# A two-layer attention and gated-MLP trunk on one core: spatial mixing with split float32r operands, output bias loaded per group

## The chip, the core and the metric

The kernel runs on one core of one Trainium2 chip. The core has five engines that run side by side: TensorE (PE, matmuls; its weight loads are listed as PEld), VectorE (DVE), ScalarE (ACT), GpSimd (POOL) and SyncE (SP, which here only issues transfers). The metric is the device time of one execution in microseconds. Before the change it is 2550.82 us, the median of three runs (2549.76 to 2550.91).

## The reference

Two layers work on x of 2048 rows by 1024 columns. Each layer projects x to 4,864 columns (queries, keys, values, gates and the gMLP halves), runs sliding-window attention on one branch and the gMLP on the other, and merges both by gates; an output projection, a residual and a LayerNorm follow. The change touches the gMLP's position mixing and the place where the output bias comes from. Of the reference that is:

```python
vn = layer_norm(v, ln_g, ln_b).reshape(B, nc, CHUNK, GMLP_GROUPS, GMLP_GROUP_DIM)
w = jnp.where(causal[None], w_s, jnp.zeros_like(w_s))
mixed = jnp.einsum('gts,bcsgd->bctgd', w, vn) + b_s.T[None, None, :, :, None]
y_g = gelu(u) * mixed * silu(z_g)
...
out = jnp.einsum('bsd,de->bse', merged, w_out[l]) + b_out[l]
x = layer_norm(ALPHA * x + out, ln_g[l], ln_b[l])
```

All data are float32. There are 4 mixing groups of 128 columns, and 16 chunks of 128 positions.

## The kernel before

The rows are worked in 4 groups of 512 (NG), each of 4 blocks of 128 (NB); both layers together make eight passes through `group(l, g, xs)`. Big products are made of float32r operands: a value is split into a high part (rounded to float32r) and a low part (the rest), and high*high, low*high and high*low are added in PSUM (`accum_t`, `accum_w`, L177 through `mm`). `hilo` does such a split: ACT casts the high part (L201), DVE subtracts it (L202). Weights arrive in units of 1024 columns. In the first group of a layer a unit is split by ACT (L136) and DVE (L137) and its two halves are kept in DRAM; in later groups the halves are loaded from there.

The order of work is the order in which the program is written, with one addition: small tasks stand in a queue (`side`), and `step` takes one after every few big matmuls (`pace`). So the attention's scores, transposes and products, and the gMLP's LayerNorm and mixing, are strewn among the matmuls of the input projection. A scheduler then orders each engine's queue; an engine works its queue strictly in that order, and a wait at its head holds everything behind it.

Position mixing of one pass: `v_norm` (L514) normalizes each of four blocks in place; then four tasks `mix_task(gi)` follow, one for each mixing group. Each takes one PSUM bank from the pool `ps_at` (3 banks, in rotation; scores and attention output use the same pool), makes four float32 matmuls (L522), and DVE evacuates the bank (L525: times `g_col`, plus `bias2`), multiplies by the gate (L530) and splits the result into the branch product's operand (`hilo`: L201, L202). The task just ahead of them, `pv_task(3)`, is the last attention product (L443), evacuated at L448.

The profile counts a float32 matmul as two records: 128 instructions at L522 show as 256.

The tiles `t` of the pool `tp` (15 buffers, in rotation) hold short-lived values of 128x512; `bo_b` (the output bias, copied to all partitions) is a constant, loaded by POOL once per layer (L254) and read at L664, where the residual is scaled.

Of the kernel before, what the change touches and what calls it, by code (L numbers as in the profile page):

```python
# [14 lines left out]
P = 128  # L15
D = 1024
# [33 lines left out]
def trunk_kernel(ctx, tc, xg, xt, wu, bcol, bvg, sinks, lngc, lnb, wsp, bsp, bout, ln_g, ln_b,  # L50
# [161 lines left out]
    sink = [const.tile([P, HEADS], F32, name=f"sink{l}") for l in range(DEPTH)]  # L212
    nsink = [const.tile([P, HEADS], F32, name=f"nsink{l}") for l in range(DEPTH)]
    vg_b = const.tile([P, GW], F32, name="vg_b")
    wsT = const.tile([P, NGR, P], F32, name="wsT")
    bias2 = const.tile([P, NGR, P], F32, name="bias2")
    bo_b = const.tile([P, D], F32, name="bo_b")
    lg_b = const.tile([P, D], F32, name="lg_b")
    lb_b = const.tile([P, D], F32, name="lb_b")
    kept = [[dram.tile([P, 2, 1024], F32, name=f"kept{l}_{n}") for n in range(NUNITS)] for l in range(DEPTH)]  # L220
# [12 lines left out]
    def mix_consts(l):  # L233
        if l > 0:
            pool.dma_start(out=vg_b, in_=bvg[l].partition_broadcast(P))
        pool.dma_start(out=wsT, in_=wsp[l])
        pool.affine_select(out=wsT, in_=wsT, pattern=[[0, NGR], [1, P]], compare_op=ALU.is_ge,
                           fill=0.0, base=0, channel_multiplier=-1)
        t = TT()
        pool.dma_start(out=t, in_=lnb[l].partition_broadcast(P))  # L240
        t2 = TT()
        pool.dma_start(out=t2, in_=bsp[l].partition_broadcast(P))

        def go():
            ps = AT([P, NGR, P])
            for gi in range(NGR):
                pe.matmul(ps[:, gi, :], lhsT=t[:, gi * P:(gi + 1) * P], rhs=wsT[:, gi, :],
                          start=True, stop=True)
            dve.tensor_tensor(out=bias2.rearrange("p g t -> p (g t)"),
                              in0=ps.rearrange("p g t -> p (g t)"), in1=t2, op=ALU.add)  # L250
        return always, go

    def out_consts(l):
        pool.dma_start(out=bo_b, in_=bout[l].partition_broadcast(P))  # L254
        pool.dma_start(out=lg_b, in_=ln_g[l].partition_broadcast(P))
        pool.dma_start(out=lb_b, in_=ln_b[l].partition_broadcast(P))

# [48 lines left out]
    def group(l, g, xs):  # L306
# [204 lines left out]

        def v_norm(b):
            def go():
                dve.tensor_scalar(out=hv[b], in0=hv[b], scalar1=mv[:, b, 0:1], scalar2=rs[:, b, :],  # L514
                                  op0=ALU.subtract, op1=ALU.mult)
            return always, go

        def mix_task(gi):
            def go():
                ps = AT([P, NB, P])  # L520
                for b in range(NB):
                    pe.matmul(ps[:, b, :], lhsT=hv[b][:, gi * P:(gi + 1) * P], rhs=wsT[:, gi, :],  # L522
                              start=True, stop=True)
                t = TT([P, NB, P])
                dve.scalar_tensor_tensor(  # L525
                    out=t, in0=ps, scalar=g_col[l][:, gi:gi + 1],
                    in1=bias2[:, gi, :].unsqueeze(1).to_broadcast([P, NB, P]),
                    op0=ALU.mult, op1=ALU.add)
                t2 = t.rearrange("p b t -> p (b t)")
                dve.tensor_tensor(out=t2, in0=t2, in1=szg[gi], op=ALU.mult)  # L530
                ys[4 + gi] = hilo(Y, t2)
# [62 lines left out]
        for b in range(NB):  # L594
            for h in range(2):
                row = g * NB + b
                src = xt[row * P:(row + 1) * P] if l == 0 else x1[g][:, b, :]
                sp.dma_start(out=rt[b][h], in_=src[:, h * T:(h + 1) * T])
        st = S([P, NB, 2, 6], "st2")
        mv = S([P, NB, 2], "mv2")  # L600
        rs = S([P, NB, 1], "rs2")
# [44 lines left out]
        for h in range(2):  # L646
# [12 lines left out]
            for u in range(1 if tail else 4):  # L659
                W = next_unit(T)  # L660
                for b in range(NB):
                    accum_w(banks[b], W, ms, u, b)
                    if u == 0:
                        dve.scalar_tensor_tensor(out=rt[b][h], in0=rt[b][h], scalar=ALPHA,  # L664
                                                 in1=bo_b[:, h * T:(h + 1) * T], op0=ALU.mult, op1=ALU.add)
            if tail:
                Ws = [next_unit(T) for _ in range(3)]
                for b in range(NB):
# [123 lines left out]
```

## Time and profile before

| What | Value |
|---|---|
| Median of three runs | 2550.82 us |
| The profiled execution | 2550.75 us |
| Its span, first to last instruction | 2549.1 us |
| Granted TensorE clock, mean over the span | 0.996 |
| TensorE busy | 2521.4 us (99%) |
| VectorE busy | 1436.6 us (56%) |
| ScalarE busy | 691.3 us (27%) |

Outside the span lie 1.65 us of the profiled execution. Matmuls overlap in the records (the end of one lies behind the start of the next), so what one costs TensorE is read from the distance of starts, and not from its duration.

### The profile page before, as it was taken

What the parts mean: (1) busy time and instruction counts of PE and PEld (TensorE: products, weight loads), DVE (VectorE), ACT (ScalarE), POOL (GpSimd) and SP (SyncE); (2) the same over time, 40 slices, a digit from 0 to 9 for tenths busy, and PEclk for the clock granted to TensorE, in tenths of its full rate; (3) what the DMA queues carried; (4) which work ended last, traced back from release to release, by engine and by line L of the source; (5) the groups of instructions that cost most, each with busy time, mean ns of one, the idle gap of its engine ahead of it and who ended that gap; (6) DMA issues with size and microseconds to landing.
All of it is one profiled execution on the core that took longest, in us unless ns stands there. A gap on an engine that the chain in (4) does not pass through costs nothing.

```text
span 2549.1 us, 32409 instructions
## 1 busy us (share of the span) xinstructions
PE 2521.4 (99%) x12176; PEld 2093.3 (82%) x12176; DVE 1436.6 (56%) x3752; ACT 691.3 (27%) x1322; POOL 431.1 (17%) x448
## 2 busy tenths in 40 slices
PE   8999999999999999999999999999999999999997
PEld 6888888888888888888878888888888888888886
DVE  7963568213782137725789577772467625586214
ACT  4443233111421114211154332421115111141110
POOL 1120041100411004210041100420003200132002
PEclk9999999999999999999999999999999999999999
DMA  8788964457554575556676897555565456655454
GB/s 322 252 293 298 330 247 168 171 192 263 201 179 169 194 264 198 186 187 222 248 273 235 292 322 287 203 180 186 212 229 200 181 183 213 235 195 179 170 196 165
DMA packets 116108, 568.39 MB, mean 223 GB/s; under 512 B 12112, under 2 KB 28528, under 8 KB 60528
## 3 DMA queue, kind: packets, MB, share of 16 engines
q1 hardware_dynamic: 109776, 546.35, 60.6%
q0 software_dynamic: 6176, 19.97, 2.2%
q8 instruction: 96, 1.57, 0.2%
q14 instruction: 60, 0.49, 0.1%
HBM read 436.25 MB, written 130.02 MB: 222 GB/s over the span
## 4 chain that ended last, share of the span: by engine, by line
PE 92%; DVE 3%; issue 2%; DMA 1%; ACT 1%; POOL 0%; SPq 0%; POOLq 0%; DVEq 0%; ACTq 0%
PE mm L177 86%; PE at L443 2%; PE at L374 2%; PE at L522 1%; DMA wr<-in_wu 1%; DVE t L288 1%; DVE w L137 1%; DVE y L664 0%; DMA b<-in_score_bias 0%; ACT y L641 0%; POOL rs L608 0%; DMA y<-in_xt 0%; DVE x L202 0%; ACT w L136 0%; SPq L264 0%
## 5 line engine op out<-in xcount | busy, mean ns | idle before, releaser
L177 PE MATMUL mm<-x,w 128*128 128x512 f32 x6528 | 1519.8, 391 | 8.6 <-ACT x L201 6.2
L177 PEld LDWEIGHTS mm<-x,w 128*128 128x128 f32 x6528 | 1220.0, 188 | 266.0 <-ACT x L201 7.0
L177 PE MATMUL mm<-y,w 128*128 128x512 f32 x1536 | 353.6, 389 | 0.0
L177 PE MATMUL mm<-w,m 128*128 128x512 f32 x1536 | 349.8, 389 | 0.2 <-DVE y L651 0.2
L177 PEld LDWEIGHTS mm<-w,m 128*128 128x128 f32 x1536 | 288.3, 188 | 60.4 <-DVE y L651 0.6
L177 PEld LDWEIGHTS mm<-y,w 128*128 128x128 f32 x1536 | 288.3, 188 | 59.7
L424 DVE STREAM_TRANSPOSE t<-t 32x128 f32<-32x128 f32 x1024 | 309.3, 302 | 14.1
L583 POOL TENSOR_TENSOR t<-t,t 128x512 f32<-128x512 f32 x64 | 85.0, 1328 | 996.8 <-DVE t L582 930.8
L137 DVE TENSOR_TENSOR w<-wr,w 128x1024 fp32r<-128x1024 f32 x108 | 148.0, 1371 | 139.7 <-ACT w L136 138.8
L551 ACT ACTIVATE t<-mm,bcol 128x512 f32<-128x512 f32 x128 | 88.2, 689 | 427.1 <-PE mm L177 427.1
L579 DVE TENSOR_TENSOR t<-t,mm 128x512 f32<-128x512 f32 x64 | 43.7, 683 | 273.4 <-PE mm L177 273.3
L177 PE MATMUL mm<-w,x 128*128 128x512 f32 x768 | 190.6, 392 | 0.0
L288 DVE STREAM_TRANSPOSE t<-t 32x128 f32<-32x128 f32 x512 | 154.9, 302 | 50.4 <-DMA t<-x 43.1
L136 ACT CAST w<-wr 128x1024 fp32r<-128x1024 f32 x108 | 113.2, 1048 | 209.9 <-DMA wr<-in_wu 114.7
L177 PEld LDWEIGHTS mm<-w,x 128*128 128x128 f32 x768 | 139.1, 189 | 25.5
L429 POOL TENSOR_SCALAR_AFFINE_SELECT t<-t 128x512 f32<-128x512 f32 x64 | 44.7, 698 | 519.4 <-DVE t L424 508.7
L201 ACT CAST m<-t 128x512 fp32r<-128x512 f32 x64 | 39.8, 621 | 291.1 <-POOL t L583 291.1
L406 ACT ACTIVATE t<-t,negm 128x128 f32<-128x128 f32 x256 | 99.3, 389 | 50.1 <-DVE negm L396 49.7
L651 DVE TENSOR_TENSOR y<-y,mm 128x512 f32<-128x512 f32 x64 | 43.9, 687 | 120.0 <-PE mm L177 120.0
L382 DVE CUSTOM_DVE_ANT_0 t<-at,b 128x256 f32<-128x256 f32 (+1 forms) x256 | 97.2, 412 | 20.8 <-PE at L374 18.0
L641 ACT ACTIVATE y<-y,nm,rs 128x512 f32<-128x512 f32 x56 | 41.1, 805 | 183.3 <-DVE nm L682 183.1
L494 ACT ACTIVATE m<-mm,bcol 128x512 f32<-128x512 f32 x64 | 44.1, 689 | 156.9 <-PE mm L177 156.7
(94 smaller groups left out, 1760.8 us busy)
## 6 DMA issues: line engine op xcount, KB each, us to landing
w<-kept SPq DMA_DIRECT2D x324, 1024.0 KB, 4.8
kept<-w SPq DMA_DIRECT2D x108, 1024.0 KB, 4.9
wr<-in_wu SPq DMA_DIRECT2D x108, 512.0 KB, 6.0
t<-in_xg SPq DMA_DIRECT2D x32, 256.0 KB, 6.1
y<-in_xt SPq DMA_DIRECT2D x32, 256.0 KB, 6.2
x<-y POOLq DMA_DIRECT2D x32, 256.0 KB, 4.7
t<-x SPq DMA_DIRECT2D x32, 256.0 KB, 5.6
y<-x SPq DMA_DIRECT2D x32, 256.0 KB, 6.4
```

The costliest lines, as they stand in the source:

```text
L136: act.copy(out=t[:, 0, :], in_=r)
L137: dve.tensor_tensor(out=t[:, 1, :], in0=r, in1=f(t)[:, 0, :], op=ALU.subtract)
L177: pe.matmul(o, lhsT=a, rhs=b, start=start, stop=stop, skip_group_check=skip)
L288: dve.transpose(out=outs[k][32 * i:32 * i + 32, :, 32 * r:32 * r + 32], in_=tiles[k][32 * r:32 * r + 32, :, 32 * i:32 * i + 32])
L374: pe.matmul(ps[:, j, :], lhsT=q[c][j][:, b * P:(b + 1) * P], rhs=KT[a][j][:, b * P:b * P + 2 * P], start=a == 0, stop=a == 1)
L382: dve.tensor_tensor_reduce(out=t[:, j, lo:], in0=ps[:, j, lo:], in1=b8[:, 2 * c + j, lo:], scale=1.0, scalar=NEG, op0=ALU.add, op1=ALU.max ...
L406: act.activation(out=w, in_=w, func=AF.Exp, bias=negm[:, bb, j:j + 1], scale=HD ** -0.5, accum_out=sums[:, bb, j:j + 1])
L424: dve.transpose(out=cur_[32 * i:32 * i + 32, :, 32 * r:32 * r + 32], in_=w[32 * r:32 * r + 32, :, 32 * i:32 * i + 32])
L429: pool.affine_select(out=prev_, in_=cur_, pattern=[[0, 4], [-1, P]], compare_op=ALU.is_gt, fill=0.0, base=0, channel_multiplier=1)
L443: pe.matmul(po[j * HD:(j + 1) * HD, b * P:(b + 1) * P], lhsT=VT[:, b + kb, j * HD:(j + 1) * HD], rhs=A["p"][b // 2][1 - kb][:, 2 * (b % 2) ...
L551: act.activation(out=t, in_=ps, func=AF.Sigmoid, bias=bias(i))
L583: pool.tensor_tensor(out=sa, in0=sa, in1=sg, op=ALU.add)
```

## The change

The mixing weights are split once per layer into a high and a low part that lie side by side (`ws2`, 4 groups of 2 x 128 columns). Each normalized block is split too (`hv[b] = hilo(M, n)`). A mixing task now makes, for each block, one float32r matmul of the block's high part with both halves of the weights (128x256, L529) and one of its low part with the high half (128x128, L531). The 128x256 results of two blocks fill a bank, so a task takes two banks of `ps_at`, where it took one, and DVE adds both halves of each bank (L534, L538), where it had one instruction. The output bias is no constant any more: each pass loads two tiles of 128x512 through the SP queue (L613) into the pool `tp`.

```diff
--- before.py
+++ after.py
@@ -212,9 +212,8 @@
     sink = [const.tile([P, HEADS], F32, name=f"sink{l}") for l in range(DEPTH)]
     nsink = [const.tile([P, HEADS], F32, name=f"nsink{l}") for l in range(DEPTH)]
     vg_b = const.tile([P, GW], F32, name="vg_b")
-    wsT = const.tile([P, NGR, P], F32, name="wsT")
+    ws2 = const.tile([P, NGR, 2, P], F32R, name="ws2")
     bias2 = const.tile([P, NGR, P], F32, name="bias2")
-    bo_b = const.tile([P, D], F32, name="bo_b")
     lg_b = const.tile([P, D], F32, name="lg_b")
     lb_b = const.tile([P, D], F32, name="lb_b")
     kept = [[dram.tile([P, 2, 1024], F32, name=f"kept{l}_{n}") for n in range(NUNITS)] for l in range(DEPTH)]
@@ -233,6 +232,7 @@
     def mix_consts(l):
         if l > 0:
             pool.dma_start(out=vg_b, in_=bvg[l].partition_broadcast(P))
+        wsT = TT([P, NGR, P])
         pool.dma_start(out=wsT, in_=wsp[l])
         pool.affine_select(out=wsT, in_=wsT, pattern=[[0, NGR], [1, P]], compare_op=ALU.is_ge,
                            fill=0.0, base=0, channel_multiplier=-1)
@@ -248,10 +248,11 @@
                           start=True, stop=True)
             dve.tensor_tensor(out=bias2.rearrange("p g t -> p (g t)"),
                               in0=ps.rearrange("p g t -> p (g t)"), in1=t2, op=ALU.add)
+            act.copy(out=ws2[:, :, 0, :], in_=wsT)
+            dve.tensor_tensor(out=ws2[:, :, 1, :], in0=wsT, in1=f(ws2)[:, :, 0, :], op=ALU.subtract)
         return always, go
 
     def out_consts(l):
-        pool.dma_start(out=bo_b, in_=bout[l].partition_broadcast(P))
         pool.dma_start(out=lg_b, in_=ln_g[l].partition_broadcast(P))
         pool.dma_start(out=lb_b, in_=ln_b[l].partition_broadcast(P))
 
@@ -511,21 +512,32 @@
 
         def v_norm(b):
             def go():
-                dve.tensor_scalar(out=hv[b], in0=hv[b], scalar1=mv[:, b, 0:1], scalar2=rs[:, b, :],
+                n = TT()
+                dve.tensor_scalar(out=n, in0=hv[b], scalar1=mv[:, b, 0:1], scalar2=rs[:, b, :],
                                   op0=ALU.subtract, op1=ALU.mult)
+                hv[b] = hilo(M, n)
             return always, go
 
         def mix_task(gi):
             def go():
-                ps = AT([P, NB, P])
-                for b in range(NB):
-                    pe.matmul(ps[:, b, :], lhsT=hv[b][:, gi * P:(gi + 1) * P], rhs=wsT[:, gi, :],
-                              start=True, stop=True)
                 t = TT([P, NB, P])
-                dve.scalar_tensor_tensor(
-                    out=t, in0=ps, scalar=g_col[l][:, gi:gi + 1],
-                    in1=bias2[:, gi, :].unsqueeze(1).to_broadcast([P, NB, P]),
-                    op0=ALU.mult, op1=ALU.add)
+                cs = slice(gi * P, (gi + 1) * P)
+                for b0 in range(0, NB, 2):
+
+                    ps = AT([P, 2, 2, P])
+                    for b in range(2):
+                        pe.matmul(ps[:, b], lhsT=hv[b0 + b][0][:, cs], rhs=ws2[:, gi], start=True,
+                                  stop=False, skip_group_check=True)
+                        pe.matmul(ps[:, b, 0, :], lhsT=hv[b0 + b][1][:, cs], rhs=ws2[:, gi, 0, :],
+                                  start=False, stop=True, skip_group_check=True)
+                    to = t[:, b0:b0 + 2, :]
+                    dve.scalar_tensor_tensor(
+                        out=to, in0=ps[:, :, 0, :], scalar=g_col[l][:, gi:gi + 1],
+                        in1=bias2[:, gi, :].unsqueeze(1).to_broadcast([P, 2, P]),
+                        op0=ALU.mult, op1=ALU.add)
+                    dve.scalar_tensor_tensor(
+                        out=to, in0=ps[:, :, 1, :], scalar=g_col[l][:, gi:gi + 1], in1=to,
+                        op0=ALU.mult, op1=ALU.add)
                 t2 = t.rearrange("p b t -> p (b t)")
                 dve.tensor_tensor(out=t2, in0=t2, in1=szg[gi], op=ALU.mult)
                 ys[4 + gi] = hilo(Y, t2)
@@ -596,6 +608,9 @@
                 row = g * NB + b
                 src = xt[row * P:(row + 1) * P] if l == 0 else x1[g][:, b, :]
                 sp.dma_start(out=rt[b][h], in_=src[:, h * T:(h + 1) * T])
+        bo_b = [TT() for _ in range(2)]
+        for h in range(2):
+            sp.dma_start(out=bo_b[h], in_=bout[l][h * T:(h + 1) * T].partition_broadcast(P))
         st = S([P, NB, 2, 6], "st2")
         mv = S([P, NB, 2], "mv2")
         rs = S([P, NB, 1], "rs2")
@@ -662,7 +677,7 @@
                     accum_w(banks[b], W, ms, u, b)
                     if u == 0:
                         dve.scalar_tensor_tensor(out=rt[b][h], in0=rt[b][h], scalar=ALPHA,
-                                                 in1=bo_b[:, h * T:(h + 1) * T], op0=ALU.mult, op1=ALU.add)
+                                                 in1=bo_b[h], op0=ALU.mult, op1=ALU.add)
             if tail:
                 Ws = [next_unit(T) for _ in range(3)]
                 for b in range(NB):
```

On TensorE, second pass of the first layer, the first mixing task among the input projection's matmuls; before (`at` is the PSUM bank, `m` a normalized block):

```order
L177 MATMUL mm_4118<-x_2571,w_3984 128x512 x2
L177 MATMUL mm_4118<-x_2572,w_3984 128x512
L522 MATMUL at_4125<-wsT,m_3438 128x128
L522 MATMUL at_4125<-wsT,m_3440 128x128
L522 MATMUL at_4125<-wsT,m_3442 128x128
L522 MATMUL at_4125<-wsT,m_3444 128x128
L177 MATMUL mm_4118<-x_2584,w_3984 128x512 x2
L177 MATMUL mm_4118<-x_2585,w_3984 128x512
```

After (`ws_103` is `ws2`; the blocks are pairs of high and low part, 4114 and 4115, 4132 and 4133, and so on):

```order
L177 MATMUL mm_4195<-x_2628,w_4041 128x512 x2
L177 MATMUL mm_4195<-x_2629,w_4041 128x512
L529 MATMUL at_4203<-ws_103,m_4114 128x256
L531 MATMUL at_4203<-ws_103,m_4115 128x128
L529 MATMUL at_4203<-ws_103,m_4132 128x256
L531 MATMUL at_4203<-ws_103,m_4133 128x128
L529 MATMUL at_4210<-ws_103,m_4145 128x256
L531 MATMUL at_4210<-ws_103,m_4146 128x128
L529 MATMUL at_4210<-ws_103,m_4157 128x256
L531 MATMUL at_4210<-ws_103,m_4158 128x128
L177 MATMUL mm_4195<-x_2641,w_4041 128x512 x2
L177 MATMUL mm_4195<-x_2642,w_4041 128x512
```

The task has kept its place between the same big matmuls; it makes eight instructions and fills two banks (4203 and 4210).

On VectorE, the same pass, from the evacuation of the last attention product (L448) on; before:

```order
L328 COPY vt<-vt 128x128
L448 TENSOR_TENSOR t_4108<-at_4091,m_3630 128x512
L525 SCALAR_TENSOR_TENSOR t_4130<-at_4125,gcol_96,bias_104 128x512
L202 TENSOR_TENSOR y_4111<-t_4108,y_4110 128x512
L530 TENSOR_TENSOR t_4130<-t_4130,m_3698 128x512
L525 SCALAR_TENSOR_TENSOR t_4149<-at_4144,gcol_96,bias_104 128x512
L202 TENSOR_TENSOR y_4134<-t_4130,y_4133 128x512
L530 TENSOR_TENSOR t_4149<-t_4149,m_3747 128x512
```

After (L449 is the same evacuation; 4203 and 4210 are the banks of the first task, 4230 and 4237 of the second):

```order
L449 TENSOR_TENSOR t_4185<-at_4168,m_3687 128x512
L534 SCALAR_TENSOR_TENSOR t_4202<-at_4203,gcol_96,bias_104 128x256
L202 TENSOR_TENSOR y_4188<-t_4185,y_4187 128x512
L538 SCALAR_TENSOR_TENSOR t_4202<-at_4203,gcol_96,t_4202 128x256
L534 SCALAR_TENSOR_TENSOR t_4202<-at_4210,gcol_96,bias_104 128x256
L538 SCALAR_TENSOR_TENSOR t_4202<-at_4210,gcol_96,t_4202 128x256
L542 TENSOR_TENSOR t_4202<-t_4202,m_3755 128x512
L534 SCALAR_TENSOR_TENSOR t_4229<-at_4230,gcol_96,bias_104 128x256
L534 SCALAR_TENSOR_TENSOR t_4229<-at_4237,gcol_96,bias_104 128x256
L202 TENSOR_TENSOR y_4219<-t_4202,y_4218 128x512
L538 SCALAR_TENSOR_TENSOR t_4229<-at_4230,gcol_96,t_4229 128x256
L538 SCALAR_TENSOR_TENSOR t_4229<-at_4237,gcol_96,t_4229 128x256
```

A bank is free when its L538 is done. That of the second task's first bank (4230) now stands behind a split's subtraction (L202) that waits for ACT.

On VectorE, first pass of the first layer, ahead of the mixing's first evacuation (L137 is a weight split, which waits for ACT's cast of the same unit; `vt` the attention's carried values); before:

```order
L137 TENSOR_TENSOR w_1586<-wr_1496,w_1586 128x1024
L137 TENSOR_TENSOR w_1622<-wr_1548,w_1622 128x1024
L328 COPY vt<-vt 128x128
L137 TENSOR_TENSOR w_1703<-wr_1590,w_1703 128x1024
L448 TENSOR_TENSOR t_1654<-at_1637,m_1118 128x512
L202 TENSOR_TENSOR y_1657<-t_1654,y_1656 128x512
L525 SCALAR_TENSOR_TENSOR t_1672<-at_1667,gcol_96,bias_104 128x512
```

After (4 normalizations at L516, here of blocks one to four, and the subtractions of their splits at L202):

```order
L137 TENSOR_TENSOR w_1588<-wr_1496,w_1588 128x1024
L516 TENSOR_SCALAR t_1600<-m_903,mv_1365,rs_1366 128x512
L516 TENSOR_SCALAR t_1613<-m_905,mv_1365,rs_1366 128x512
L516 TENSOR_SCALAR t_1625<-m_907,mv_1365,rs_1366 128x512
L202 TENSOR_TENSOR m_1603<-t_1600,m_1602 128x512
L137 TENSOR_TENSOR w_1639<-wr_1550,w_1639 128x1024
L202 TENSOR_TENSOR m_1616<-t_1613,m_1615 128x512
L202 TENSOR_TENSOR m_1628<-t_1625,m_1627 128x512
L516 TENSOR_SCALAR t_1647<-m_909,mv_1365,rs_1366 128x512
L329 COPY vt<-vt 128x128
L202 TENSOR_TENSOR m_1650<-t_1647,m_1649 128x512
L137 TENSOR_TENSOR w_1741<-wr_1592,w_1741 128x1024
```

Before, the normalizations stood further up, ahead of the attention's transposes. Now they stand between the weight splits next to the mixing; the subtraction of the fourth block (1650) is the last one, behind a weight split and two subtractions that wait for ACT.

## Rows read from the trace of the kernel before

**Rows 1.** The page: busy time, share of the span, instructions

```profile
PE 2521.4 (99%) x12176; PEld 2093.3 (82%) x12176; DVE 1436.6 (56%) x3752; ACT 691.3 (27%) x1322; POOL 431.1 (17%) x448
```

**Rows 2.** Timeline of TensorE, pass two: start us, us, line, operation, count

```profile
471.90 1.05 PE L522 MATMUL at<-wsT,m 128*128 128x128 f32 x8
472.71 1.85 PE L177 MATMUL mm<-x,w 128*128 128x512 f32 x7
474.40 1.05 PE L522 MATMUL at<-wsT,m 128*128 128x128 f32 x8
...
476.66 1.05 PE L522 MATMUL at<-wsT,m 128*128 128x128 f32 x8
...
479.96 10.69 PE L177 MATMUL mm<-x,w 128*128 128x512 f32 x46
490.49 11.04 PE L177 MATMUL mm<-y,w 128*128 128x512 f32 x48
501.37 9.00 PE L177 MATMUL mm<-x,w 128*128 128x512 f32 x39
```

**Rows 3.** Timeline of TensorE, scores of the second layer, float32r, 256 columns

```profile
1304.47 0.28 PE L374 MATMUL at<-ka,m 128*128 128x256 f32 x1
...
1304.94 2.23 PE L177 MATMUL mm<-x,w 128*128 128x512 f32 x9
```

**Rows 4.** Weight loads by form: shapes, count | busy us, mean ns | idle

```profile
L443 PEld LDWEIGHTS at<-t,vt 128*64 128x64 f32 x1024 | 55.2, 137 | 11.3 <-issue 7.8 <-POOL t L429 1.8 <-POOL t L431 1.8
...
L522 PEld LDWEIGHTS at<-wsT,m 128*128 128x128 f32 x256 | 33.5, 191 | 2.5
```

**Rows 5.** VectorE by form, same columns

```profile
L525 DVE SCALAR_TENSOR_TENSOR t<-at,gcol,bias 128x512 f32<-128x512 f32 x32 | 23.9, 748 | 11.6 <-PE at L522 11.6
...
L530 DVE TENSOR_TENSOR t<-t,m 128x512 f32<-128x512 f32 x32 | 22.0, 688 | 0.9
...
L626 DVE SCALAR_TENSOR_TENSOR y<-y,mv,lg_b 128x256 f32<-128x256 f32 x2 | 1.0, 479 | 0.0
```

**Rows 6.** ScalarE by form, same columns

```profile
L201 ACT CAST y<-t 128x512 fp32r<-128x512 f32 x64 | 39.7, 620 | 150.2 <-DVE t L448 100.3 <-DVE t L530 49.8
```

**Rows 7.** Timeline of VectorE, pass two

```profile
472.99 0.75 DVE L525 SCALAR_TENSOR_TENSOR t<-at,gcol,bias 128x512 f32<-128x512 f32 x1 [1.77 <-PE at L522]
473.66 0.68 DVE L202 TENSOR_TENSOR y<-t,y 128x512 fp32r<-128x512 f32 x1
```

**Rows 8.** Window, pass two: PE, PEld, DVE, ACT, POOL busy, clock, DMA

```profile
458.00:469.00 11.00, 11.00 (x55) 8.93 (x55) 0.00 (x1) 1.51 (x3) 2.57 (x2) 1.00 0.53 192
```

**Rows 9.** Timeline of VectorE, pass one

```profile
157.63 1.22 DVE L137 TENSOR_TENSOR w<-wr,w 128x1024 fp32r<-128x1024 f32 x1 [3.52 <-ACT w L136]
...
162.25 1.22 DVE L137 TENSOR_TENSOR w<-wr,w 128x1024 fp32r<-128x1024 f32 x1 [3.26 <-ACT w L136]
163.39 0.68 DVE L448 TENSOR_TENSOR t<-at,m 128x512 f32<-128x512 f32 x1
```

**Rows 10.** Timeline of TensorE, pass one

```profile
159.85 1.05 PE L522 MATMUL at<-wsT,m 128*128 128x128 f32 x8
...
162.12 1.05 PE L522 MATMUL at<-wsT,m 128*128 128x128 f32 x8
```

**Rows 11.** Timeline of VectorE, pass five (first of the second layer)

```profile
1423.94 0.68 DVE L448 TENSOR_TENSOR t<-at,m 128x512 f32<-128x512 f32 x1
```

**Rows 12.** Timeline of TensorE, pass five

```profile
1424.67 1.05 PE L522 MATMUL at<-wsT,m 128*128 128x128 f32 x8
```

**Rows 13.** Timeline of TensorE, start of the second layer

```profile
1295.10 0.39 PE L374 MATMUL at<-ka,m 128*128 128x256 f32 x1 [1.96 <-DVE m L462]
...
1297.16 0.58 PE L374 MATMUL at<-ka,m 128*128 128x256 f32 x1 [1.56 <-DVE m L462]
```

**Rows 14.** Window around that place, same columns

```profile
1295.00:1320.00 25.00, 23.34 (x107) 19.65 (x108) 23.44 (x72) 13.59 (x29) 9.39 (x11) 0.86 0.91 332
```

**Rows 15.** DMA issues: out<-in, engine, count, KB each, median us to landing

```profile
bo_b<-in_bout POOLq DMA_DIRECT2D x2, 512.0 KB, 6.7
```

## The prediction, made before the changed kernel ran

> **What bounds the kernel now.** I read the page's table of engines first: TensorE is busy for 99% of the span, no other engine for more than 56% [rows 1]. So the time is TensorE's work plus its few waits, and a change is worth what it does to the one or the other; work on VectorE or ScalarE counts only where TensorE comes to wait for it. Next I read TensorE's timeline around one pass's mixing, for prices by distance of starts. Forty-eight big matmuls take 501.37 - 490.49 = 10.88 us, 0.2267 us each. From the first mixing record (471.90) to 490.49 lie 18.59 us with four mixing tasks and 7, 6, 7 and 46 big matmuls; 66 x 0.2267 = 14.96 us, and 3.63 us remain, 0.907 us a task or 0.113 us for each of its eight records [rows 2]. There are 32 tasks (8 passes of 4), 29 us in all.
>
> **What the change does to TensorE's work.** A task's eight float32 records become four float32r matmuls of 256 columns and four of 128. The first kind stands in the trace, as the scores: four take 1304.94 - 1304.47 = 0.47 us, 0.1175 us each [rows 3]. The second, a float32r matmul of 128 columns, does not. Below, it could cost half of the 256-column one, 0.059 us. Above, it could cost as much as the whole float32 matmul of this size, two records, 0.227 us. Between them is the float32 record itself, which has the same columns and the same 128x128 weights: 0.113 us. Loads of weights speak for that middle: a load of 64 columns is recorded with 137 ns and one of 128 with 191 ns [rows 4], so 64 columns more are 54 ns, and 128 columns are by estimate 108 ns of loading. Each small matmul still needs a load of its own, and a matmul can't follow faster than the loads do. I take 0.113. The task is then 4 x (0.1175 + 0.113) = 0.92 us, against 0.907: +0.5 us in 32 tasks. At 0.059 it is 0.706 us (-6.4 us in all), at 0.227 it is 1.378 us (+15.1 us).
>
> The Trainium skill speaks against this middle: "TensorE: Matmul & The Clock Gate", section "Back-to-back issue gap", gives some 81 ns for a matmul of 128 columns in a stream of load and matmul pairs. By it the task would be 4 x (117.5 + 81) = 794 ns, 3.6 us less than now in 32 tasks. The float32 records at 113 ns can't decide it, as they may be slow by their type and not by their loads; no row here is a float32r one of this size.
>
> **What it adds on VectorE and ScalarE.** Before, a task's VectorE work is 0.748 + 0.688 us and a subtraction of about the same 0.69 [rows 5, 7]: 2.13 us. Now the 0.748 becomes four instructions of 128x256. The nearest row of that size and kind takes 0.479 us from SBUF [rows 5], and half of 0.748 would be 0.374; I take 0.48, so the task is 3.30 us. With the split of the blocks (one subtraction each) VectorE gets 32 x (1.17 + 0.69) = 60 us more, ScalarE 32 casts of 0.620 us, 20 us [rows 6]. In most of a pass that is hidden: VectorE does nothing from 458 to 469 us, just before the mixing [rows 8], and in pass two the normalizations and casts fit there. What isn't hidden is the speed of evacuation. TensorE reaches a task every 2.3 to 2.5 us (474.40 - 471.90, 476.66 - 474.40) [rows 2]. VectorE's 3.30 us, with a wait for ScalarE's cast between multiplication and subtraction, is slower than that. Before, a task took one bank of three; now it takes two. So the second bank of the third task is the first of the second task, and the second bank of the second task the first of the first.
>
> **The waits, place by place.** An instruction on VectorE follows some 0.08 us before the end recorded for the one ahead (473.66 after 472.99 + 0.75) [rows 7], and some 0.1 us after it where it needs its result (my estimate). Pass two: the first bank is full at about 472.54 and evacuation begins. By the order shown above it goes L534, subtraction, L538, L534, L538, multiplication, to 475.8 us; then two L534 for the second task and a subtraction that waits for a cast until 476.5; the L538 that frees its first bank ends at 477.6. TensorE wants that bank 0.46 us into its third task, at 476.66 + 0.46 = 477.1 [rows 2]. It waits 0.5 us. The fourth task's banks are free in time. Six passes run like this: 3.0 us.
>
> Pass one is worse, as weights are split there. VectorE's weight split begins at 157.63 [rows 9]; by the new order two subtractions, the fourth normalization, a cast and the last subtraction stand behind it: 158.8, 160.0, 160.7, 161.3, 162.05. TensorE, which begins the first task at 159.85, needs that last low part at 160.66 [rows 10] and waits 1.4 us. The second task comes at 163.8 then, but the evacuation of the last attention product, which stands behind the weight split and now frees the bank of this task and not of the third, ends at about 164.2 (before: 163.39 + 0.68 [rows 9]): 0.4 us. Its second bank waits for the first L538, behind a cast and a subtraction, until 166.0, where TensorE arrives at 164.7: 1.3 us. The third task's second bank: about 1.0. Together 4.1 us. Pass five has the same pattern with the evacuation at 1423.94 + 0.68 = 1424.62 [rows 11] and the second task at 1424.67 [rows 12]: nothing for the first bank, 1.3 us for the second, 1.2 us in the third task, 2.5 us. In all 3.0 + 4.1 + 2.5 = 9.6 us.
>
> These waits are bounded from both sides. With evacuations of 0.374 us, and casts that come a little earlier, they are gone but for pass one, near zero in all. If VectorE's whole task counts, 3.30 us and 0.7 us for the cast, it loses 1.6 us on TensorE's 2.4 for each of the last two tasks: 8 x 3.2 = 26 us. If the small matmul costs more, TensorE comes later and waits less.
>
> **The rest, costed at nothing.** The bias: 16 loads of 256 KB on SP's queue behind or between the residual's loads; a load twice that size landed in 6.7 us [rows 15]. VectorE's residual scaling waits for it, with weight splits and the next pass's operands behind it. TensorE needs the scaled residual only after 96 big matmuls, 21.8 us, and a weight unit is split two units ahead, 48 matmuls, 10.9 us. Both are longer than a landing. Without that cover it is at most some 3 us in passes one and five. SP's weight loads stand behind two short issues more. POOL loses two loads that nothing waits for. The split of the mixing weights is one cast and one subtraction a layer, under other work. Four more `t` tiles shift the pool's rotation; what they replace has long been read.
>
> **Sum.** Against the profiled execution, 2550.75 us, which is the median (2550.82) but for 0.07: + 0.5 + 9.6 = 2560.9; I say 2561.
>
> **Rivals.**
> 1. VectorE keeps up. It is free in over four tenths of the span [rows 1], and my waits are a few tenths of a microsecond each, worked out from durations that are partly estimates. Against it: in pass one the evacuation at 163.39 is already later than the task it must now serve. Price: 2550.75 + 0.5, about 2551.
> 2. The small float32r matmul is dear, 0.227 us. For it: no row shows one, and float32 matmuls are listed as two records. Against it: at 256 columns float32r runs at half the price of 512, so nothing but columns seems to count. Time: 2550.75 + 15.1 + about 4 of waits, which shrink as TensorE's task grows by 0.47 us: 2570.
> 3. The waits bring the clock down. At the start of the second layer two waits of 1.96 and 1.56 us within four microseconds stand [rows 13] in a window with a granted clock of 0.86 [rows 14], that is, a part of it at 1.2 instead of 2.4 GHz: 0.14 x 25 = 3.5 us. Pass one's waits are shorter and more spread. If both first passes fall: 2561 + 7 = 2568.
> 4. Faster: the small matmul costs its columns alone, 0.059 us, and 6.4 us go. It decides only where waits stay under 1.3 us; then about 2546. With my waits, which grow little, it is 2554. The skill's 81 ns would lie between this and the forecast: 2557.
>
> **Chances.** Forecast 0.42; VectorE keeps up 0.15; dear small matmul 0.15; clock 0.10; cheap small matmul 0.18, in half of which waits are gone. A measurement of this kernel can tell 0.2%, 5.1 us, from no change. Slower: 0.42 + 0.15 + 0.10 = 0.67. The same: 0.15 + 0.09 = 0.24. Faster: 0.09. The range is 2550 to 2571: it takes in the rivals of 2551, 2554, 2568 and 2570, and leaves out a gain and the upper bound of the waits.
>
> **What would show it.** Right: rows of L529 and L531 whose distance of starts is near 0.12 and 0.11 us; VectorE's L538 named as what ended TensorE's idle time at L529, about once a pass, some 10 us in all, most in passes one and five; a wait for L202 at the first task of pass one; no new window with a lower clock. Wrong: L531 at 0.06 or at 0.22 us from its successor, or TensorE without waits at L529, or its new waits at the output projection behind the bias.

## The result, and the profile after

The changed kernel takes 2563.99 us (median of four runs, 2563.87 to 2564.38). The kernel before, timed beside it, takes 2550.63 us; the ratio is 1.0055 with a 95% interval of 1.0043 to 1.0067. That is slower, by 13.4 us or 0.55%. The profiled execution of the changed kernel took 2564.09 us, with a span of 2562.3 us; that of before had a span of 2549.1, so some 13.2 us are to be found.

The engines, from the page; it answers to [rows 1]:

```profile
PE 2525.2 (99%) x12176; PEld 2096.0 (82%) x12176; DVE 1487.2 (58%) x3882; ACT 709.5 (28%) x1356; POOL 432.3 (17%) x446
```

VectorE has 51 us more and TensorE 4 us; of these totals neither says where the 13 us went. What says it is the start of each pass's first mixing record, after against before. From one such record to the next a pass has grown by:

| pass | 1 | 2 | 3 | 4 | 5 | 6 | 7 | 8 |
|---|---|---|---|---|---|---|---|---|
| us more | 2.56 | 0.62 | 0.86 | 1.27 | 5.37 | 1.04 | 1.03 | 0.88 |

(A column reaches from one pass's mixing to the next one's, so the output projection of the pass is in it. Until the first such record the changed kernel is 0.35 us ahead; 13.63 - 0.35 = 13.28.) Every pass loses something, the first pass of each layer (one and five) most, and pass five much more than pass one.

The groups of the mixing, by form (busy us, mean ns, idle time just before and what ended it); L534 and L538 answer to L525 in [rows 5]:

```profile
L529 PE MATMUL at<-ws,m 128*128 128x256 f32 x128 | 32.5, 323 | 6.7 <-DVE t L538 6.7
L538 DVE SCALAR_TENSOR_TENSOR t<-at,gcol,t 128x256 f32<-128x256 f32 x64 | 30.1, 480 | 0.6
L534 DVE SCALAR_TENSOR_TENSOR t<-at,gcol,bias 128x256 f32<-128x256 f32 x64 | 29.9, 477 | 2.6 <-PE at L531 2.6
L531 PE MATMUL at<-ws,m 128*128 128x128 f32 x128 | 28.4, 222 | 0.0
```

TensorE's idle time at the mixing is all before L529 and all ended by L538, the second evacuation of a bank. Each evacuation of 128x256 takes 0.48 us. The 323 and 222 ns of the matmuls are no prices: these records overlap. Prices are distances of starts, from TensorE's timeline in pass two, tasks one to three (answering to [rows 2]):

```profile
474.11 0.28 PE L529 MATMUL at<-ws,m 128*128 128x256 f32 x1
474.22 0.22 PE L531 MATMUL at<-ws,m 128*128 128x128 f32 x1
474.28 0.34 PE L529 MATMUL at<-ws,m 128*128 128x256 f32 x1
474.45 0.22 PE L531 MATMUL at<-ws,m 128*128 128x128 f32 x1
474.51 0.34 PE L529 MATMUL at<-ws,m 128*128 128x256 f32 x1
...
476.63 0.28 PE L529 MATMUL at<-ws,m 128*128 128x256 f32 x1
...
478.93 0.28 PE L529 MATMUL at<-ws,m 128*128 128x256 f32 x1
...
479.28 0.22 PE L531 MATMUL at<-ws,m 128*128 128x128 f32 x1
479.75 0.35 PE L529 MATMUL at<-ws,m 128*128 128x256 f32 x1 [0.26 <-DVE t L538]
```

A pair of L529 and L531 takes 474.51 - 474.28 = 0.23 us. The first two tasks, with the same big matmuls between them, lie 2.52 and 2.30 us apart, where they lay 2.50 and 2.26 apart before. So a task costs TensorE 0.02 to 0.04 us more, about 1 us in 32 tasks. In the third task the second bank comes late: 479.75 - 479.28 = 0.47 us, where 0.06 is usual. Counted so (distance from L531 to the next L529, less 0.06), the waits at the mixing are 2.2 us in pass one, 0.4, 0.6 and 0.9 in passes two to four, 1.7 in pass five and 0.8 in each of the last three: 8.4 us.

VectorE in the same stretch (columns as in [rows 7]):

```profile
474.71 0.48 DVE L534 SCALAR_TENSOR_TENSOR t<-at,gcol,bias 128x256 f32<-128x256 f32 x1 [1.29 <-PE at L531]
475.11 0.68 DVE L202 TENSOR_TENSOR y<-t,y 128x512 fp32r<-128x512 f32 x1
475.71 0.48 DVE L538 SCALAR_TENSOR_TENSOR t<-at,gcol,t 128x256 f32<-128x256 f32 x1
...
478.53 0.68 DVE L202 TENSOR_TENSOR y<-t,y 128x512 fp32r<-128x512 f32 x1
479.13 0.87 DVE L538 SCALAR_TENSOR_TENSOR t<-at,gcol,t 128x256 f32<-128x256 f32 x2
```

From the first evacuation on no idle time stands in VectorE's rows, those left out included. The pair of L538 that begins at 479.13 frees the second task's banks, about 0.4 us apiece; TensorE goes on at 479.75. It is the instruction that the forecast named.

Pass one, TensorE and then VectorE (answering to [rows 9, 10]):

```profile
159.50 0.28 PE L529 MATMUL at<-ws,m 128*128 128x256 f32 x1
...
160.37 1.59 PE L177 MATMUL mm<-x,w 128*128 128x512 f32 x6
...
163.66 0.36 PE L529 MATMUL at<-ws,m 128*128 128x256 f32 x1 [1.19 <-DVE t L538]
...
167.08 0.35 PE L529 MATMUL at<-ws,m 128*128 128x256 f32 x1 [0.70 <-DVE t L538]
```

```profile
154.28 1.23 DVE L137 TENSOR_TENSOR w<-wr,w 128x1024 fp32r<-128x1024 f32 x1 [0.55 <-ACT w L136]
...
157.85 0.69 DVE L202 TENSOR_TENSOR m<-t,m 128x512 fp32r<-128x512 f32 x1 [0.55 <-ACT m L201]
159.91 1.23 DVE L137 TENSOR_TENSOR w<-wr,w 128x1024 fp32r<-128x1024 f32 x1 [1.37 <-ACT w L136]
161.06 0.68 DVE L449 TENSOR_TENSOR t<-at,m 128x512 f32<-128x512 f32 x1
```

The first task runs without a break (159.50 to 160.37): the last low part was done at 158.5. The weight splits run at 154.28 and 159.91 here, and not at 157.63 and 162.25 as before [rows 9], and so L449 came 2.3 us earlier too. The lead begins some 40 us ahead of that place. Before, the four normalizations stood ahead of a weight split:

```profile
112.55 2.54 DVE L514 TENSOR_SCALAR m<-m,mv,rs 128x512 f32<-128x512 f32 x4 [1.16 <-POOL rs L509]
115.01 1.22 DVE L137 TENSOR_TENSOR w<-wr,w 128x1024 fp32r<-128x1024 f32 x1
```

After, they have moved back, and that split runs 3.1 us earlier:

```profile
111.93 1.22 DVE L137 TENSOR_TENSOR w<-wr,w 128x1024 fp32r<-128x1024 f32 x1
```

The splits behind it keep a lead of 2.3 to 3.4 us.

What the forecast did not have stands in pass five, at the output projection. TensorE, then two windows on it (us, PE, PEld, DVE, ACT, POOL busy, clock, DMA), then VectorE's transposes of the next pass's input (L289), residual scalings (L679) and first evacuation (L666):

```profile
1580.45 5.75 PE L177 MATMUL mm<-w,m 128*128 128x512 f32 x17 [2.14 <-DVE y L666]
```

```profile
1575.00:1580.60 5.60, 3.46 (x16) 2.57 (x15) 5.37 (x13) 0.30 (x1) 0.00 (x0) 1.00 0.76 256
1580.70:1584.00 3.30, 3.30 (x9) 2.52 (x9) 3.21 (x7) 1.16 (x2) 0.00 (x0) 0.50 0.98 310
```

```profile
1509.07 5.04 DVE L289 STREAM_TRANSPOSE t<-t 32x128 f32<-32x128 f32 x16
...
1559.27 0.67 DVE L679 SCALAR_TENSOR_TENSOR y<-y,t 128x512 f32<-128x512 f32 x1
1559.87 0.61 DVE L289 STREAM_TRANSPOSE t<-t 32x128 f32<-32x128 f32 x2
...
1561.20 9.51 DVE L289 STREAM_TRANSPOSE t<-t 32x128 f32<-32x128 f32 x30
...
1579.71 0.69 DVE L666 TENSOR_TENSOR y<-y,mm 128x512 f32<-128x512 f32 x1
```

TensorE stands for over 2 us until L666 frees a bank, and the 3.4 us behind that wait are granted 0.50, that is 1.2 GHz instead of 2.4. The transposes stop at 1514.1, start again at 1559.87, and fill VectorE until the evacuation. Before, they ran in pieces from 1537.89 on, and the first evacuation of that stage was at 1570.96.

### The profile page after: what moved, and what is told of

Same layout as the page of the kernel before. It is cut to its first block, busy times and chain, and to the rows that moved or that the text cites. A ratio compares the mean times of both kernels' runs of the same rounds, so it can differ in the third digit from the quotient of the medians.

```text
span 2562.3 us, 32669 instructions
## 1 busy us (share of the span) xinstructions
PE 2525.2 (99%) x12176; PEld 2096.0 (82%) x12176; DVE 1487.2 (58%) x3882; ACT 709.5 (28%) x1356; POOL 432.3 (17%) x446
## 4 chain that ended last, share of the span: by engine, by line
PE 83%; DVE 9%; DMA 3%; issue 3%; ACT 1%; POOL 0%; SPq 0%; DVEq 0%; POOLq 0%; ACTq 0%
PE mm L177 79%; DMA wr<-in_wu 2%; DVE t L425 2%; PE at L375 2%; PE at L444 2%; DVE w L137 2%; DVE t L289 1%; DVE t L538 1%; DVE y L202 1%; DVE t L534 1%; ACT w L136 0%; DVE t L412 0%; DMA t<-in_xg 0%; PE at L529 0%; ACT y L201 0%
## 5 line engine op out<-in xcount | busy, mean ns | idle before, releaser
L137 DVE TENSOR_TENSOR w<-wr,w 128x1024 fp32r<-128x1024 f32 x108 | 148.9, 1378 | 127.3 <-ACT w L136 126.5
L289 DVE STREAM_TRANSPOSE t<-t 32x128 f32<-32x128 f32 x512 | 154.9, 302 | 50.2 <-DMA t<-x 43.0
L202 DVE TENSOR_TENSOR m<-t,m 128x512 fp32r<-128x512 f32 x96 | 70.3, 744 | 123.0 <-ACT m L201 122.4
L201 ACT CAST m<-t 128x512 fp32r<-128x512 f32 x96 | 58.0, 620 | 295.3 <-POOL t L595 287.6
L666 DVE TENSOR_TENSOR y<-y,mm 128x512 f32<-128x512 f32 x64 | 43.6, 683 | 103.3 <-PE mm L177 103.3
```

Of the source, the lines that this page charges most:

```text
L137: dve.tensor_tensor(out=t[:, 1, :], in0=r, in1=f(t)[:, 0, :], op=ALU.subtract)
L201: act.copy(out=h, in_=src)
L202: (lo_engine or dve).tensor_tensor(out=o, in0=src, in1=f(h), op=ALU.subtract)
L289: dve.transpose(out=outs[k][32 * i:32 * i + 32, :, 32 * r:32 * r + 32], in_=tiles[k][32 * r:32 * r + 32, :, 32 * i:32 * i + 32])
```

## Experiments

Nine kernels were run, each timed beside the kernel before. Theory R, on pass five, is that the two tiles of the bias are in the way in pool `t`. Theory V, on the mixing, is that the waits are VectorE's time per bank. The diffs are shortened: keyword names and some arguments are left out, and the move of the bias is shown once.

**The bias in a buffer of its own.**

```diff
-        bo_b = [TT() for _ in range(2)]       # per pass, in pool t
+            bo_b = bop.tile([P, T], F32, ...)  # per half, pool of one buffer
```

> The changed kernel, with the bias of each half of the output projection in a pool of its own with one buffer, so that it takes no slot in the rotation of the t tiles. Theory R (the two bias tiles shift the rotation, the late transposes of pass five stand still for 46 us and then run as a block in front of the evacuations): the wait of 2.53 us at 1577.9 and the half clock of 3.41 us behind it vanish, some 3.6 to 3.9 us come back, about 2560. Rival L (the bias lands late, or VectorE is simply too loaded with the new evacuations of the mixing): the wait stays, about 2564. The waits at the mixing (8.4 us in all) stay with either.

Measured: 2560.43 us, ratio 1.0044 [1.0031, 1.0056]; 3.6 us less than the changed kernel (2.9 us less when each is taken against the kernel before that was timed beside it, with intervals that overlap; the two profiled spans, 2562.3 and 2558.4 us, lie 3.9 apart). TensorE and VectorE at the place (transposes are L290 here):

```profile
1569.75 10.59 PE L178 MATMUL mm<-w,m 128*128 128x512 f32 x46
```

```profile
1544.94 2.19 DVE L290 STREAM_TRANSPOSE t<-t 32x128 f32<-32x128 f32 x7
...
1565.24 6.03 DVE L290 STREAM_TRANSPOSE t<-t 32x128 f32<-32x128 f32 x19
1575.39 0.68 DVE L666 TENSOR_TENSOR y<-y,mm 128x512 f32<-128x512 f32 x1
```

Forty-six big matmuls run without a break, the transposes begin at 1544.94 again, and no clock falls there. The start of pass six comes 3.8 us earlier than in the changed kernel, that of pass five 0.1: all of the gain is in pass five. Theory R holds. The run also moves the issue of the load, to the start of each half; the pool and the place of the issue were not tried apart.

**The bias alone moved, mixing as before.** The kernel before with the two `t` tiles per pass.

> The kernel before, with only the bias moved: two t tiles per pass, loaded at the output projection; the mixing is float32 as before. Theory R (the rotation alone does it): a wait of some 2.5 us at the output projection of pass five with a fall of the clock, about 2554. Rival L (the load of the mixing on VectorE is needed as well): no wait there, about 2550.7.

Measured: 2553.85 us, ratio 1.0014 [1.0006, 1.0023]. TensorE at the output projection of pass five:

```profile
1572.73 6.64 PE L177 MATMUL mm<-w,m 128*128 128x512 f32 x20 [2.68 <-DVE y L652]
```

The wait is there, with the granted clock at 0.5 from 1574.2 for 3.4 us, and the mixing has nothing to do with it. That the bias lands late is refuted by the run before this one: with the own buffer VectorE waits for its landing more (25.9 us in all, the longest 8.3, against 11.8 and 4.6 in the changed kernel), and TensorE does not wait at that place. How the tiles act can be read from VectorE's program. In the changed kernel it has in pass five, from the last of five splits of transposed tiles on (`t_1804` is a tile of the bias):

```
L202 TENSOR_TENSOR x_1827_12765<-t_1753_12355,x_1826_12764 128x512
...
L679 SCALAR_TENSOR_TENSOR y_1798_12670<-y_1798_12670,t_1804_12684 128x512
L137 TENSOR_TENSOR w_1822_12742<-wr_1791_12633,w_1822_12742 128x1024
L202 TENSOR_TENSOR m_1795_12665<-t_1779_12555,m_1794_12664 128x512
L679 SCALAR_TENSOR_TENSOR y_1800_12672<-y_1800_12672,t_1804_12684 128x512
L289 STREAM_TRANSPOSE t_1828_12776<-t_1742_12268 32x4x32 x2
L679 SCALAR_TENSOR_TENSOR y_1802_12674<-y_1802_12674,t_1804_12684 128x512
L289 STREAM_TRANSPOSE t_1828_12776<-t_1742_12268 32x4x32 x14
L289 STREAM_TRANSPOSE t_1833_12837<-t_1752_12345 32x4x32 x16
```

With the bias in its own pool the sixth tile's transposes stand right behind those splits. So from 1514 to 1559 us they are not held by a transfer (no idle time stands before the row of 1559.87); they stand behind the residual scalings in VectorE's order, and the order comes out so when the bias takes tiles of this pool. It is not that a buffer comes free late: by the built program the sixth tile takes the buffer of a tile that the split (L202) at 1525.72 read last, 33 us earlier. But it takes its buffer after the two tiles of the bias, and in the program its first transpose stands right behind the issue of the second bias load. SP makes that issue behind the residual's eight loads:

```profile
1550.23 3.96 SPq L610 DMA_DIRECT2D y<-x  x8
1554.42 0.33 SPq L613 DMA_DIRECT2D t<-in_bout  x1
```

The kernel of this experiment has the same order. That the transposes stand late because their tile is asked for after those of the bias is argued from the program; no run asks for the tiles in another order.

**ScalarE takes one half of each bank.**

```diff
-                    dve.scalar_tensor_tensor(to, ps[:, :, 0, :], g, bias2, mult, add)
-                    dve.scalar_tensor_tensor(to, ps[:, :, 1, :], g, to, mult, add)
+                    act.activation(to, ps[:, :, 1, :], Identity, scale=g)
+                    dve.scalar_tensor_tensor(to, ps[:, :, 0, :], g, to, mult, add)
+                dve.tensor_tensor(t, t, bias2, add)      # once per task
```

> The changed kernel, with the product of the low weights taken out of each bank by ScalarE (scaled by g), VectorE adding the other half of the bank, and one VectorE addition of the bias per task of 512 columns. Theory V (the waits at the mixing are VectorE's time per bank, two passes of 0.48 us each): VectorE has one pass per bank and one of 512 per task, and waits of 8.4 us fall to 3 to 5 us, about 2559 to 2561. Rival B (the two banks per task are too many for the three buffers, or ScalarE's cast is late, whoever empties them): they stay or grow, 2564 to 2568.

Measured: 2563.18 us, ratio 1.0053 [1.0039, 1.0067]: the time speaks for neither theory. The places do. In passes two to four and six to eight no distance of starts at the mixing is over 0.3 us, where the changed kernel loses 4.5 us. In passes one and five the waits have grown (TensorE, pass five):

```profile
1436.99 0.36 PE L529 MATMUL at<-ws,m 128*128 128x256 f32 x1 [1.95 <-DVE t L536]
```

and 3.4 us at a clock of 0.5 follow. The wait at the output projection of pass five is there too, 3.4 us from start to start, with no fall of the clock behind it. So V holds in the six passes, though two banks per task are the same. In the first pass of a layer it is again VectorE's half of the bank that ends the wait; the rows are shown below, at the run with ScalarE in all passes and the bias in its own buffer.

**The three products summed in TensorE, one bank per task.**

```diff
+                    pe.matmul(ps[:, b, :], lhsT=h, rhs=ws2[:, gi, 0, :], start=True, stop=False)
+                    pe.matmul(ps[:, b, :], lhsT=h, rhs=ws2[:, gi, 1, :], start=False, stop=False)
+                    pe.matmul(ps[:, b, :], lhsT=o, rhs=ws2[:, gi, 0, :], start=False, stop=True)
```

> The changed kernel with the three products of a batch element summed in TensorE: twelve float32r matmuls of 128 columns into one bank per task, and one evacuation of 512 as before the change. It separates the price of a 128-column float32r matmul from the waits. At 0.113 us each a task is 1.36 us, +14 us over 32 tasks against the kernel before, no waits at the mixing: with the bias's 4 us about 2569. At 0.06 us a task is 0.72 us, 6 us less than before: about 2549. At 0.227 us a task is 2.7 us: over 2600.

Measured: 2566.89 us, ratio 1.0066 [1.0054, 1.0079], close to the 2569 of the middle price. TensorE, pass two, L528 to L530 the three products:

```profile
472.47 0.22 PE L528 MATMUL at<-ws,m 128*128 128x128 f32 x1
472.52 0.28 PE L529 MATMUL at<-ws,m 128*128 128x128 f32 x1
472.64 0.27 PE L530 MATMUL at<-ws,m 128*128 128x128 f32 x1
...
475.44 0.22 PE L528 MATMUL at<-ws,m 128*128 128x128 f32 x1
```

But for the first, they follow each other by 0.11 us; tasks lie 2.97 us apart instead of 2.50 [rows 2]. There is no wait at the mixing. The wait of pass five's output projection stays (2.74 us from start to start), as the bias is in pool `t`; but no fall of the clock follows it, so that 1.7 of the 4 us set down for the bias did not come.

**Without the second evacuation.** Own buffer for the bias, L538 left out.

> The bias in its own buffer, and the evacuation of the low weights' product (L538) left out, so that part of the sum is missing: two VectorE instructions of 128x256 less per task, TensorE's work and its two banks per task as in the changed kernel. The waits at the mixing there are 8.6 us in all. Theory V (VectorE's time per bank): they go, 2560.4 - 8.6 = about 2552, what remains over the kernel before is TensorE's 1 us of longer tasks. Rival B (two banks per task of three, whatever VectorE takes): more than half of the waits stays, 2556 or more.

Measured: 2553.61 us, ratio 1.0011 [1.0002, 1.0020]; 6.8 us less than with L538. The group of L530 (L529 before), by form:

```profile
L530 PE MATMUL at<-ws,m 128*128 128x256 f32 x128 | 31.8, 324 | 1.8 <-DVE t L535 1.3 <-DVE t L450 0.3
```

In the six passes nothing is left. Some 1.4 us in pass one and 1.6 in pass five stay, behind the splits and the attention's evacuation. Theory V holds for the six, and for most of the rest.

**And without the low parts' matmul.** L531 left out as well.

> As the run before this one, and the 128-column matmul of the blocks' low parts (L531) left out as well, another part of the sum: TensorE makes four float32r matmuls of 256 columns per task and nothing else. It measures what the small matmul costs when VectorE holds nothing up. Theory K (it costs its weight load, some 0.113 us): 128 x 0.113 = 14.5 us less than the run before, about 2537.5. Rival C (it costs its columns, 0.058 us as the distance to its successor shows): 7.4 us less, about 2544.5.

Measured: 2540.09 us, ratio 0.9959 [0.9947, 0.9972]; 13.5 us less than the run before it, near the 14.5 of theory K. Tasks lie 2.09 us apart (with L531: 2.52):

```profile
472.24 0.64 PE L530 MATMUL at<-ws,m 128*128 128x256 f32 x4
...
474.33 0.64 PE L530 MATMUL at<-ws,m 128*128 128x256 f32 x4
```

So a small matmul costs 0.43/4 = 0.11 us, though its successor starts only 0.06 us after it. The distance to one neighbour misleads; that over the pair, 0.23 us, doesn't.

**ScalarE in the later passes alone.** The two evacuations as changed where `g == 0`, ScalarE's half elsewhere, bias in its own buffer.

> The bias in its own buffer, and ScalarE taking half of each bank in passes two to four and six to eight alone; in the first pass of each layer, where ScalarE and VectorE also split weights, VectorE takes both halves as in the changed kernel. Theory V: the six passes' waits (some 4.9 us) go, those of the two first passes stay: 2560.4 - 4.9 = about 2555.5. If ScalarE's extra work delays another step in those passes, as rival A has it: 2558 or more.

Measured: 2556.36 us, ratio 1.0024 [1.0014, 1.0035], 0.9 over theory V's number. Waits stay in passes one and five only. It is the fastest here with all three float32r products, and still slower than the kernel before.

**ScalarE in all passes, own buffer.**

> ScalarE takes half of each bank in all passes, and the bias has its own buffer. If the two effects add up: what ScalarE gave (2563.2 against 2564.0) and what the own buffer gave (3.5 us) together, about 2559.5. Rival A (in the first passes of a layer the waits are ScalarE's, whose casts of split weights and blocks stand in the same queue, so that they stay at 4 us or more there while those of the other six are nil): the time is the same 2559 to 2560 but the waits stand in passes one and five alone. Rival V2 (VectorE alone counts everywhere): no waits there either, 2553.

Measured: 2558.75 us, ratio 1.0033 [1.0021, 1.0046]: the time and the places are those of rival A, with 3.8 us of waits in the tasks of passes one and five each, and none elsewhere. Its reason is not what the rows show. The longer wait of pass five, up to 1438.25, is for the first bank of the third task. ScalarE, then VectorE:

```profile
1435.19 0.48 ACT L535 ACTIVATE t<-at,gcol 128x256 f32<-128x256 f32 x1
```

```profile
1435.89 1.22 DVE L138 TENSOR_TENSOR w<-wr,w 128x1024 fp32r<-128x1024 f32 x1
...
1437.63 1.26 DVE L537 SCALAR_TENSOR_TENSOR t<-at,gcol,t 128x256 f32<-128x256 f32 x3
```

ScalarE is done with its half at 1435.67. VectorE comes to the other half at 1437.63, without idle time but behind a weight split and a subtraction. So here too the wait is set by VectorE's order, and not by ScalarE's queue. The shorter wait, 1.3 us, also ends with VectorE's half, behind a subtraction that waits 0.69 us for ScalarE's cast.

**One rounded product.** The runs above say that TensorE's work is what is left to take away: the kernel before, with normalized blocks and weights rounded to float32r.

```diff
+                hv[b] = M()                     # float32r, written by the normalization
-                    pe.matmul(ps[:, b, :], ..., rhs=wsT[:, gi, :], ...)
+                    pe.matmul(ps[:, b, :], ..., rhs=wsR[:, gi, :], ...)
```

> The kernel before, with the mixing as one float32r product: normalized blocks and weights are rounded to float32r once and both low parts are left out, so the products are less exact. No split of blocks, one bank and one VectorE evacuation per task as before, bias constant as before. TensorE makes four float32r matmuls of 128 columns per task, each with a load of its own. Theory K (a load of 128 columns sets the pace, 0.111 to 0.113 us): a task is 0.45 us against 0.907, 14.6 us less than the kernel before, about 2536. Rival C (columns set it, 0.058 us): 0.23 us a task, 21.6 us less, about 2529. In either case no waits at the mixing and none at the output projection.

Measured: 2543.07 us, ratio 0.9970 [0.9959, 0.9981]: faster than both kernels, for less exact products, but by half of what was expected. The price was right: tasks lie 2.05 us apart, 0.45 less than before, 14.4 us in all. What was given back is in passes one and five (TensorE, then VectorE, pass five):

```profile
1422.42 1.12 PE L526 MATMUL at<-wsR,m 128*128 128x128 f32 x4 [3.59 <-DVE t L450]
```

```profile
1420.54 1.23 DVE L137 TENSOR_TENSOR w<-wr,w 128x1024 fp32r<-128x1024 f32 x1 [3.90 <-ACT w L136]
1421.68 0.68 DVE L450 TENSOR_TENSOR t<-at,m 128x512 f32<-128x512 f32 x1
```

The last attention product (L450) stands behind a weight split that waits 3.90 us for ScalarE's cast. A faster TensorE only comes to the bank sooner: 3.7 us more here, 1.5 in pass one, and 6.8 us at half the clock from 1421.4, which cost 3.4. Together that is 8.6 of the 14.4 us; 2.2 us of the gain in the profiled run lie ahead of the first mixing record and are not the mixing's. "No waits at the mixing" was wrong. The run without low parts has the same waits (2.3 and 1.3 us), and no fall of the clock behind them. A version with that evacuation ahead of the split was not tried.

## Why the prediction was right, and where it was not

The direction, the time (2561 forecast, 2564 measured) and the main mechanism came out; that the time came so near is in part luck, as the sum at the end shows. Step by step:

- **TensorE's work, +0.5 us.** It is about +1 (0.02 to 0.04 us a task). The small matmul at 0.113 is measured with 0.11, by leaving it out and by twelve of them in a row. Rivals 2 and 4 (0.227, 0.059) fall. That the loads of the weights set it fits the 108 ns worked out from [rows 4], but no run changes a load alone. "L531 at 0.06 or at 0.22 us from its successor" was named as a sign of being wrong, and 0.06 is what the rows have (474.45 to 474.51). The sign was ill chosen: there are 0.17 us ahead of L531, and the pair has the 0.23 that was forecast. The Trainium skill's 81 ns ("TensorE: Matmul & The Clock Gate", section "Back-to-back issue gap") isn't borne out in this kernel: float32r matmuls of 128 columns go at 0.11 us, in a row as well. Another section of that page of the Trainium skill, "LDWEIGHTS (loading the stationary operand)", has a load take its columns divided by 1.2, in ns, by estimate 107 for 128 columns; the 0.106 to 0.111 us measured per small matmul agree with it.
- **VectorE's 0.48 us per evacuation** is 0.477 and 0.480, and L538 is what ends TensorE's waits. Rival 1 falls. In all VectorE has 51 us more where 60 were forecast, and ScalarE 18 where 20 were.
- **The waits at the mixing, 9.6 us,** are 8.4, but not as laid out. The six later passes have 4.5 instead of 3.0: pass two was worked out with 0.5 and has 0.4, and its price was carried to passes that have 0.6 to 0.9. In pass four and in six to eight the wait stands in the fourth task, whose banks the forecast had free in time; in pass six, for one, a subtraction that waits for ScalarE stands ahead of the first evacuation. Pass five has 1.7 instead of 2.5, and pass one 2.2 instead of 4.1. There the 1.3 and 1.0 us at the second banks came (1.35 and 0.86), but the 1.4 us for the fourth low part and the 0.4 for the second task's first bank did not. The forecast put the weight split of 157.63 [rows 9] ahead of that low part and kept its time, but the split of that place in the new order ran at 154.28, as the four normalizations no longer stood in front of it. An order was read with the times of another one. Smaller: the 0.1 us by which an instruction was estimated to follow one whose result it needs is 0.03 on VectorE (163.43 + 0.48 to 163.94, L534 and L538 in pass one).
- **"The rest, costed at nothing" failed**, in its last sentence: "Four more `t` tiles shift the pool's rotation; what they replace has long been read." The new tiles are six a pass and not four: four for the normalized blocks and two for the bias. At the place in pass five what they replace had long been read indeed; what the sentence left out is that the order of the pool's other users moves with them. The two of the bias cost 3.6 us, all in pass five, with the bound (3 us in passes one and five) close in size but for another reason. The landing of the bias, which the bound was on, cost nothing that can be seen: VectorE's L679 waits for it 11.8 us, three times, and TensorE doesn't. New waits at the output projection stood among the forecast's own signs of being wrong, and one came.
- **Rival 3, the clock,** came at that place and not at the mixing: 3.4 us at 0.50, 1.7 us lost, part of the 3.6.

The sum as measured: 1.0 + 8.4 + 3.6 = 13.0 of 13.2 us. The forecast's 10.1 lacked the 3.6, and an overshoot of 1.2 on the waits hid part of it; in that 1.2 in turn 1.5 us too little in six passes stand against 2.7 too much in the other two.

## What to carry to other kernels

A float32r matmul of 128 columns cost 0.11 us here, and one of 256 columns 0.12, so count the matmuls, each with a load of its own, before the columns. Where a task takes more banks, ask how long the evacuating engine needs per bank, and what stands ahead of it in that engine's order. When a change moves instructions on an engine, the times of those that stood behind them move too, and must not be carried over from the old trace. A tile moved from a constant into a shared pool is not free: give it a buffer of its own, or look where the order of that pool's users has moved.

## What was not expected of the hardware

A float32r matmul of 128 columns between ones of 256 is followed after 0.06 us, one among others of 128 after 0.11; only the sum over a pair is a price. Waits counted from start to start: single ones of 1.4 us at the mixing left the granted clock at 1.00 (window of pass one, 158 to 170 us), while one of 2.5 us at the output projection was followed by 3.4 us at 0.50, and one of 4.0 us at the mixing (one rounded product) went with 6.8 us. But 2.5 us in the run without low parts, 2.7 us in the run with one bank, and 3.4 us at the output projection of the run in which ScalarE takes half were followed by no such stretch. The plainest pair is the same wait of 2.4 us in pass five of the two runs with ScalarE in all passes: with the bias in pool `t` 3.4 us at 0.50 follow, with its own buffer none. So the length of the wait alone doesn't decide it.
